# Reordering the start of a transformer-layer kernel: column groups, features and first products in the order in which their data lands

## The chip, the cores and the metric

The kernel runs on one core of one Trainium2 chip. The metric is the device time of one execution in microseconds; the time before is the median of three runs. The engines are TensorE (PE, with its weight loads listed as PEld), VectorE (DVE), ScalarE (ACT), GpSimd (POOL) and SyncE (SP), which issues the DMAs.

## The reference

One layer works on 512 latent tokens `x` and 256 context tokens `ctx`, both of width 1024, in f32. Only the new `x` is returned.

```python
mod   = silu(c)     @ w_ada + b_ada        # per channel shift, scale, gate for x
mod_c = silu(c_ctx) @ w_ada + b_ada        # the same for ctx
h  = rms_norm(x,   g_norm1) * (1 + sc1)  + sh1
hc = rms_norm(ctx, g_norm1) * (1 + csc1) + csh1
aq, ak, av, dq, dk, dv, dz, da, db, ga, gd = split_cols(h  @ w_in)
caq, cak, ...                              = split_cols(hc @ w_in)
...   # windowed attention and gated DeltaNet, merged, output projection, MLP
```

What matters here is the beginning: the modulation columns, the two norms, the modulated features `h` and `hc`, and the first column tiles of the product with `w_in`.

## The kernel before

Tokens lie along the free axis and channels along the partitions: the width of 1024 is eight channel tiles of 128 partitions, `kt` = 0 to 7. A product of one 128-column tile of `w_in` with all tokens is a sum over the eight channel tiles, over 512 columns of `x` and 256 of `ctx`. To keep f32 accuracy, weights and features are each split in a rounded upper part and a remainder, and `mm3` multiplies three pairs (L309 upper with upper, L310 upper with remainder, L311 remainder with upper). The split of a weight is `wload`: a DMA to a raw buffer (L251), the upper part on ScalarE (L256), the remainder on VectorE (L261). The raw buffers are two, so a third load waits until the first is split.

The start consists of these pieces:

- 36 warm-up matmuls of a tile of ones (L198), whose result nobody reads.
- For each channel tile the column group `ada(kt)`: two halves of 512 KB of `w_ada` are loaded (L215), and four small matmuls each (L217) form the rows of scale and shift. `columns(kt)` copies them (L231, ScalarE), turns them into columns (L236, TensorE) and adds the bias (L244, L245, VectorE) to get `modA` and `modS`. For tile 0 another 14 matmuls without a use stand behind it (L240).
- The norms: for `x` and then `ctx`, squares on ScalarE (L285), sums on VectorE (L289, L293), a sum over partitions as a matmul with ones (L296), and a logarithm and an exponent on ScalarE (both L156 through `act`). The program has all squares, then both exponents.
- The features of a channel tile, `modulate`: a product on VectorE (L314), the rounded upper part on ScalarE (L315), the remainder on VectorE (L316), for `x` and then for `ctx`.
- Three early weights (`load_early`: the gate tile and two key tiles), whose products are formed channel tile by channel tile as features come (`early`), into six of the eight banks of accumulation memory.

The instructions are not run in the order in which the program is written. A scheduler orders those of each engine by priority and readiness in its own estimate and sets the semaphores; the resulting order of every engine is fixed before the run, and each engine waits in it. An order can be forced by adding a dependency without a semaphore. SP issues DMAs in order too, and an issue also waits until the DMA eight places ahead of it has landed.

Behind the early products come the other tiles of `w_in` out of a queue of weights (`wnext`), with the gate steps, convolution, norms, attention and DeltaNet work in between, then merge, output projection and MLP.

## Time and profile before

| | |
|---|---|
| median of 3 runs | 920.05 us (916.64 to 921.29) |
| profiled execution | 919.03 us, span 917.3 us |
| mean granted TensorE clock | 0.996 |
| TensorE busy | 892.9 us, 97% of the span |
| VectorE, ScalarE, GpSimd busy | 648.8, 497.5, 26.0 us |

The span runs from the first to the last instruction; the execution's time holds 1.7 us more. In a timeline row stand the start, the duration, the engine, the line, the operation with output and inputs, and how many instructions the row merges; in brackets the idle time ahead of it and what ended it. Matmul durations overlap, since matmuls are pipelined; the distance of two starts is what one costs. A 128-column f32 matmul with an f32 operand counts as two rows. In the view of stretches stand the stretch, its length and for each engine its busy time with the number of instructions, then the granted TensorE clock (1.00 is full), the DMA engines' busy share and GB/s.

### The profile page before, as it was taken

Reading aid. Unit: us, or ns where it says so; the run is one execution under the profiler, and the core shown is the slowest. Engines: PE = TensorE matmul, PEld = TensorE weight load, DVE = VectorE, ACT = ScalarE, POOL = GpSimd, SP = SyncE. Lnnn points to the kernel's source line nnn. Section 1 sums busy time; section 2 is a strip of 40 time slices with the busy share of each in tenths; the row PEclk is TensorE's granted clock in tenths of the full one; section 3 lists DMA queues with packets and bytes.
Section 4 is the critical chain, followed back from the end, with each engine's and each line's share of the span. In section 5 each row is a group of like instructions: output and inputs, shape, how many; then the busy total and the mean of one; then the engine's idle time right before and its main releaser. Section 6 shows DMA issues by size and latency. Waiting matters only on the chain.

```text
span 917.3 us, 19321 instructions
## 1 busy us (share of the span) xinstructions
PE 892.9 (97%) x8228; PEld 748.7 (82%) x8228; DVE 648.8 (71%) x1100; ACT 497.5 (54%) x873; POOL 26.0 (3%) x42
## 2 busy tenths in 40 slices
PE   8999999999999999999999999999999999999998
PEld 6688677877777777878878889888899899889986
DVE  4665799966777998357787967997587477637731
ACT  5468755457768787485545425563265146414520
POOL 0000001010000001000000000000000000000000
PEclk9999999999999999999999999999999999999999
DMA  8914345442212133324455555453412340233031
GB/s 343 346 47 116 74 107 111 103 93 47 58 28 43 47 105 115 97 72 163 139 174 179 184 177 184 141 181 114 138 47 93 115 160 27 90 113 117 25 115 46
DMA packets 31910, 107.19 MB, mean 117 GB/s; under 512 B 3920, under 2 KB 4432, under 8 KB 31824
## 3 DMA queue, kind: packets, MB, share of 16 engines
q1 hardware_dynamic: 29520, 97.57, 31.4%
q0 software_dynamic: 2304, 8.39, 5.6%
q8 instruction: 64, 1.05, 0.5%
q14 instruction: 22, 0.18, 0.1%
HBM read 103.85 MB, written 2.10 MB: 116 GB/s over the span
## 4 chain that ended last, share of the span: by engine, by line
PE 81%; DVE 8%; ACT 7%; issue 2%; DMA 2%; SPq 0%; ACTq 0%; DVEq 0%
PE banks L309 14%; PE banks L310 14%; PE banks L311 14%; PE banks L988 11%; PE banks L1436 11%; PE banks L1034 2%; PE banks L1099 2%; ACT m L156 2%; PE banks L1111 1%; DMA m<-in_wm 1%; PE banks L1130 1%; PE banks L573 1%; DVE m L193 1%; PE banks L636 1%; PE banks L744 1%
## 5 line engine op out<-in xcount | busy, mean ns | idle before, releaser
L309 PE MATMUL banks<-m,wh 128*128 128x512 f32 (+1 forms) x568 | 212.8, 376 | 0.1
L310 PE MATMUL banks<-m,wh 128*128 128x512 f32 (+1 forms) x568 | 211.1, 372 | 0.0
L311 PE MATMUL banks<-m,wl 128*128 128x512 f32 (+1 forms) x568 | 210.8, 371 | 0.0
L256 ACT ACTIVATE wh<-wr 128x1024 fp32r<-128x1024 f32 (+1 forms) x92 | 90.5, 985 | 134.0 <-PE banks L310 113.1
L1436 PE MATMUL banks<-m,m 128*128 128x256 f32 x1008 | 123.6, 284 | 1.8 <-DVE m L193 1.0
L1436 PEld LDWEIGHTS banks<-m,m 128*128 128x128 f32 x1008 | 121.9, 192 | 3.6 <-DVE m L193 1.7
L311 PEld LDWEIGHTS banks<-m,wl 128*128 128x128 f32 x568 | 107.3, 189 | 18.8 <-issue 0.8
L309 PEld LDWEIGHTS banks<-m,wh 128*128 128x128 f32 x568 | 107.3, 189 | 18.5 <-ACT m L156 0.5
L192 ACT ACTIVATE m<-m 128x512 fp32r<-128x512 f32 (+2 forms) x118 | 82.5, 720 | 73.2 <-PE banks L1436 13.4
L310 PEld LDWEIGHTS banks<-m,wh 128*128 128x128 f32 x568 | 107.4, 189 | 17.5 <-DVE m L193 0.3
L193 DVE TENSOR_TENSOR m<-m,m 128x512 fp32r<-128x512 f32 (+2 forms) x118 | 92.3, 804 | 21.4 <-ACT m L192 16.8
L988 PE MATMUL banks<-m,wh 128*128 128x512 f32 x320 | 104.4, 400 | 0.6 <-ACT m L156 0.6
L261 DVE TENSOR_TENSOR wl<-wr,wh 128x1024 fp32r<-128x1024 f32 (+1 forms) x76 | 84.2, 1109 | 26.2 <-ACT wh L256 24.0
L1563 DVE SCALAR_TENSOR_TENSOR m<-banks,modT,m 128x512 f32<-128x512 f32 x32 | 24.0, 749 | 77.7 <-PE banks L311 77.7
L988 PEld LDWEIGHTS banks<-m,wh 128*128 128x128 f32 x320 | 59.3, 188 | 13.0 <-ACT m L156 0.8
L988 PE MATMUL banks<-m,wl 128*128 128x512 f32 x160 | 64.5, 403 | 0.0
L1053 DVE SCALAR_TENSOR_TENSOR m<-m,m 128x1024 f32<-128x1024 f32 x32 | 38.9, 1219 | 12.3 <-DMA m<-in_wada 12.2
L310 PE MATMUL banks<-m,m 128*128 128x256 f32 (+1 forms) x136 | 46.1, 346 | 0.1
L309 PE MATMUL banks<-m,m 128*128 128x256 f32 (+1 forms) x136 | 44.9, 344 | 1.2 <-ACT m L256 0.6
L311 PE MATMUL banks<-m,m 128*128 128x256 f32 (+1 forms) x136 | 44.8, 338 | 0.1
L988 PEld LDWEIGHTS banks<-m,wl 128*128 128x128 f32 x160 | 30.1, 188 | 6.2
L156 ACT ACTIVATE m<-banks,st 128x512 f32<-128x512 f32 (+1 forms) x32 | 23.5, 738 | 20.1 <-DVE st L530 19.8
(256 smaller groups left out, 1382.2 us busy)
## 6 DMA issues: line engine op xcount, KB each, us to landing
m<-in_wada SPq DMA_DIRECT2D x48, 512.0 KB, 5.0
wr<-in_wm SPq DMA_DIRECT2D x40, 512.0 KB, 3.4
wr<-in_win SPq DMA_DIRECT2D x39, 512.0 KB, 3.3
m<-in_wm SPq DMA_DIRECT2D x24, 512.0 KB, 3.4
wl<-in_win POOLq DMA_DIRECT2D x16, 512.0 KB, 5.5
m<-in_xT SPq DMA_DIRECT2D x8, 512.0 KB, 5.4
wr<-in_wbr SPq DMA_DIRECT2D x16, 256.0 KB, 2.7
wr<-in_wout SPq DMA_DIRECT2D x8, 512.0 KB, 3.3
```

Source lines behind the costliest of these rows:

```text
L156: r = A.activation(out_, in_, func, **kw)
L192: A.activation(r32(hi), src, AF.Copy)
L193: (eng or V).tensor_tensor(r32(lo), src, hi, op=ALU.subtract)
L256: A.activation(r32(hi), raw, AF.Copy)
L261: V.tensor_tensor(r32(lo), raw, hi, op=ALU.subtract)
L309: PE.matmul(acc, w[0][:, k, :], xhi, start=(start and i == 0), stop=False)
L310: PE.matmul(acc, w[0][:, k, :], xlo, start=False, stop=False)
L311: PE.matmul(acc, w[1][:, k, :], xhi, start=False, stop=(stop and i == n - 1))
L988: PE.matmul(acc.ap, w[x][:, k, :], hx[k][y], start=(k == p == 0), stop=(k == KT - 1 and p == 2))
L1053: V.scalar_tensor_tensor(wa.ap, wa.ap, 0.5, scr.ap, op0=ALU.mult, op1=ALU.mult, accum_out=modT[:, grp, j:j + 1])
L1436: PE.matmul(dst, r32(self.w[w][i][:, k * P:(k + 1) * P]), xs7[x][k][j], start=(n == 0), stop=(n == 11))
L1563: V.scalar_tensor_tensor(xn_[ct], accs[ct].ap, modT[:, 3, ct:ct + 1], xn_[ct], op0=ALU.mult, op1=ALU.add)
```

## The change

The same work is written in another order, with fewer warm-ups, and a few orders are forced.

- The warm-ups are 30 and 8 instead of 36 and 14.
- The DMA of the first early weight is issued ahead of those of `ctx`, and its upper part on ScalarE is forced behind the exponent of `x`.
- The norm of `x` is finished, exponent included, before the norm of `ctx`; the squares of `ctx` on ScalarE are forced behind the first rounded feature of `x`.
- Each partition sum of a norm is forced behind the column group's matmuls issued last.
- The feature of `x` of channel tile 0 is made ahead of column group 1, and the first early product of `x` (three matmuls) is placed behind it; the second partition sum is forced behind that product. Features of `ctx` are made once its norm is there.

```diff
-NONES, NWAIT = 36, 14
+NONES, NWAIT = 30, 8
...
+    def follow(later, earlier):
+
+        tc.add_manual_dep(later.ins, earlier.ins.name, nosync, reason="order")
...
-                PE.matmul(rp_[32 * g:32 * g + 32, :256], scond[:, half * 4 + g], wb[:, g * 256:(g + 1) * 256],
-                          start=(half == 0), stop=(half == 1))
+                last[0] = PE.matmul(rp_[32 * g:32 * g + 32, :256], scond[:, half * 4 + g], wb[:, g * 256:(g + 1) * 256],
+                                    start=(half == 0), stop=(half == 1))
...
-            PE.matmul(mp[:, half, :], rb_[:, half * P:(half + 1) * P], prm[:, 184:186], start=True, stop=True)
+            last[0] = PE.matmul(mp[:, half, :], rb_[:, half * P:(half + 1) * P], prm[:, 184:186], start=True, stop=True)
...
-        A.activation(r32(hi), raw, AF.Copy)
+        upper[0] = A.activation(r32(hi), raw, AF.Copy)
...
-    columns(0, ada(0))
+    rp0 = ada(0)
+    load_early()
+    w0 = upper[0]
     for k4 in range(KT // 4):
         nc.sync.dma_start(out=cs_[:, k4 * 1024:(k4 + 1) * 1024], in_=I["ctxT"][k4])
-    load_early()
...
-    for src, nt, n, r in ((xs_, 4, SEQ, rx), (cs_, 2, CTX, rc)):
+    def norm1(src, nt, n, r, sq_after=None):
         tot = None
         for i in range(nt):
             b = alloc(1024)
-            A.activation(b.ap, src[:, i * 1024:(i + 1) * 1024], AF.Square)
+            q = A.activation(b.ap, src[:, i * 1024:(i + 1) * 1024], AF.Square)
+            if sq_after:
+                follow(q, sq_after)
...
-        PE.matmul(ss[:, :n], ones, tot[:, :n], start=True, stop=True)
+        follow(PE.matmul(ss[:, :n], ones, tot[:, :n], start=True, stop=True), last[0])
         tot.free()
         act(r, ss[:, :n], AF.Ln, bias=epsc, scale=1.0 / D)
         ss.free()
-    for r in (rx, rc):
-        act(r, r, AF.Exp, scale=-0.5)
...
+        return act(r, r, AF.Exp, scale=-0.5)
...
-    for kt in range(1, AHEAD):
-        columns(kt, ada(kt))
-        load_early()
-    for kt in range(KT):
+
+    def features(kt):
+
         t = alloc(768)
         o, oc = kt * 1024, kt * 512
-        hx.append(modulate(t[:, :512], xt[kt], rx, modA[:, kt, 0:1], modS[:, kt, 0:1],
-                           H[:, o:o + 512], H[:, o + 512:o + 1024]))
-        hc.append(modulate(t[:, 512:768], ct_[kt], rc, modA[:, kt, 1:2], modS[:, kt, 1:2],
-                           HCb[:, oc:oc + 256], HCb[:, oc + 256:oc + 512]))
+        if len(hx) == kt:
+            hx.append(modulate(t[:, :512], xt[kt], rx, modA[:, kt, 0:1], modS[:, kt, 0:1],
+                               H[:, o:o + 512], H[:, o + 512:o + 1024]))
+        if len(normed) == 2:
+            hc.append(modulate(t[:, 512:768], ct_[kt], rc, modA[:, kt, 1:2], modS[:, kt, 1:2],
+                               HCb[:, oc:oc + 256], HCb[:, oc + 256:oc + 512]))
         t.free()
+
+    def early_x(w, acc, k):
+        return mm3(acc[:, :512], w, [hx[k]], start=(k == 0), stop=(k == KT - 1), ks=[k])
+
+
+    normed = [norm1(xs_, 4, SEQ, rx)]
+    follow(w0, normed[0])
+    columns(0, rp0)
+    features(0)
+    hi0 = upper[0]
+    columns(1, ada(1))
+    load_early()
+    low0 = early_x(*early[0], 0)
+    follow(low0, last[0])
+    last[0] = low0
+    normed.append(norm1(cs_, 2, CTX, rc, hi0))
+    for kt in range(KT):
+        features(kt)
         if kt + AHEAD < KT:
             columns(kt + AHEAD, ada(kt + AHEAD))
         if len(early) < len(EARLY):
             load_early()
         for (w, acc), k0 in zip(early, EARLY.values()):
             for k in range(kt + 1) if kt == k0 else (kt,):
-                mm3(acc[:, :512], w, [hx[k]], start=(k == 0), stop=(k == KT - 1), ks=[k])
+                if k or acc is not early[0][1]:
+                    early_x(w, acc, k)
                 mm3(acc[:, 512:768], w, [hc[k]], start=(k == 0), stop=(k == KT - 1), ks=[k])
```

`mm3` and `modulate` are moved up unchanged, except that `mm3` returns its last matmul and `modulate` remembers its ScalarE instruction in `upper`; `last` and `upper` hold the instruction issued last of their kind. The line numbers in the prediction are those of the kernel before.

More of the change, by code (lines that the diff above doesn't have):

```diff
@@ L216, in ada @@
             for g in range(4):
-                PE.matmul(rp_[32 * g:32 * g + 32, :256], scond[:, half * 4 + g], wb[:, g * 256:(g + 1) * 256],
-                          start=(half == 0), stop=(half == 1))
+                last[0] = PE.matmul(rp_[32 * g:32 * g + 32, :256], scond[:, half * 4 + g], wb[:, g * 256:(g + 1) * 256],
+                                    start=(half == 0), stop=(half == 1))
             wb.free()
         return rp_
+    last = [None]
     xs_, cs_ = alloc(8 * SEQ), alloc(8 * CTX)
@@ L246, in columns @@
         mp_.free()
+    upper = [None]
     def wload(src, n=KT, bufs=None, late=False):
@@ L270, in load_early, with mm3, modulate @@
         early.append((wload(I["win"][list(EARLY)[len(early)]], bufs=bb), bank(2)))
-    columns(0, ada(0))
+    def mm3(acc, w, xs, start=True, stop=True, ks=None):
+        ks = list(range(len(xs))) if ks is None else ks
+        n = len(ks)
+        for i, k in enumerate(ks):
+            xhi, xlo = xs[i]
+            PE.matmul(acc, w[0][:, k, :], xhi, start=(start and i == 0), stop=False)
+            PE.matmul(acc, w[0][:, k, :], xlo, start=False, stop=False)
+            r = PE.matmul(acc, w[1][:, k, :], xhi, start=False, stop=(stop and i == n - 1))
+        return r
+    def modulate(t, src, r, sc, sh, hi, lo, eng=V):
+        V.scalar_tensor_tensor(t, src, sc, r, op0=ALU.mult, op1=ALU.mult)
+        upper[0] = A.activation(r32(hi), t, AF.Identity, bias=sh)
+        eng.scalar_tensor_tensor(r32(lo), t, sh, hi, op0=ALU.add, op1=ALU.subtract)
+        return r32(hi), r32(lo)
+    rp0 = ada(0)
+    load_early()
+    w0 = upper[0]
     for k4 in range(KT // 4):
         nc.sync.dma_start(out=cs_[:, k4 * 1024:(k4 + 1) * 1024], in_=I["ctxT"][k4])
-    load_early()
     xt = [xs_[:, k * SEQ:(k + 1) * SEQ] for k in range(KT)]
@@ L299, in tile_layer @@
         ss.free()
-    for r in (rx, rc):
-        act(r, r, AF.Exp, scale=-0.5)
-    def mm3(acc, w, xs, start=True, stop=True, ks=None):
-        ks = list(range(len(xs))) if ks is None else ks
-        n = len(ks)
-        for i, k in enumerate(ks):
-            xhi, xlo = xs[i]
-            PE.matmul(acc, w[0][:, k, :], xhi, start=(start and i == 0), stop=False)
-            PE.matmul(acc, w[0][:, k, :], xlo, start=False, stop=False)
-            PE.matmul(acc, w[1][:, k, :], xhi, start=False, stop=(stop and i == n - 1))
@@ L313, in modulate @@
-    def modulate(t, src, r, sc, sh, hi, lo, eng=V):
-        V.scalar_tensor_tensor(t, src, sc, r, op0=ALU.mult, op1=ALU.mult)
-        A.activation(r32(hi), t, AF.Identity, bias=sh)
-        eng.scalar_tensor_tensor(r32(lo), t, sh, hi, op0=ALU.add, op1=ALU.subtract)
-        return r32(hi), r32(lo)
+        return act(r, r, AF.Exp, scale=-0.5)
     H, HCb = alloc(8 * 1024, True), alloc(8 * 512, True)
     hx, hc = [], []
-    for kt in range(1, AHEAD):
-        columns(kt, ada(kt))
-        load_early()
```

## The prediction

> **What bounds the kernel now.** I read the page first (the engines' shares, the chain that ended last), then the busy time by stretches of the first 60 us, then the timeline there; and beside them the order in which each engine holds its instructions in the two programs.

> ```profile
> span 917.3 us, 19321 instructions
> PE 892.9 (97%) x8228; PEld 748.7 (82%) x8228; DVE 648.8 (71%) x1100; ACT 497.5 (54%) x873; POOL 26.0 (3%) x42
> PE 81%; DVE 8%; ACT 7%; issue 2%; DMA 2%; SPq 0%; ACTq 0%; DVEq 0%
> ```

> TensorE is busy for 97% of the span and carries 81% of the chain. So a change off TensorE pays only where TensorE has nothing to do, and that is the start:

> ```profile
> 10.00:15.00 5.00, 3.75 (x32) 1.93 (x30) 2.59 (x3) 1.62 (x4) 0.00 (x0) 1.00 1.02 419
> 20.00:25.00 5.00, 3.79 (x24) 1.48 (x16) 2.44 (x7) 2.23 (x5) 0.00 (x0) 1.00 0.91 330
> 25.00:30.00 5.00, 5.00 (x31) 2.87 (x31) 3.10 (x5) 2.49 (x5) 0.00 (x0) 0.66 1.01 412
> 28.00:29.00 1.00, 1.00 (x10) 0.52 (x3) 0.10 (x1) 0.38 (x2) 0.00 (x0) 0.50 1.00 410
> ```

> The columns after the stretch are PE, PEld, DVE, ACT, POOL, then granted clock, DMA share, GB/s. Weight loads fill only 1.48 of the 5 us from 20 on: TensorE waits there. From about 26 to 29 us it ran at half clock. At 419 GB/s a transfer of 512 KB takes 1.25 us. Nothing later differs: behind the first features and their products all engines hold the same instructions in the same order in both programs. The whole effect is how much earlier TensorE becomes continuously busy with needed work.

> The timeline of before's start, engine by engine:

> ```profile
> 1.06 10.45 PE L198 MATMUL banks<-ones 128*128 128x128 f32 x72 [1.06 <-DVE ones L166]
> 9.57 1.06 ACT L285 ACTIVATE m<-m 128x1024 f32<-128x1024 f32 x1 [0.15 <-DMA m<-in_xT]
> 11.44 0.64 PE L217 MATMUL banks<-m,m 128*32 128x256 f32 x8
> 12.88 1.10 PE L296 MATMUL banks<-m,ones 128*128 128x512 f32 x2 [0.80 <-DVE m L293]
> 13.90 0.64 PE L217 MATMUL banks<-m,m 128*32 128x256 f32 x8
> 14.01 0.69 ACT L156 ACTIVATE m<-banks,epsc 128x512 f32<-128x512 f32 x1 [3.38 <-PE banks L296]
> 14.61 0.38 ACT L231 ACTIVATE m<-banks 128x256 f32<-128x256 f32 x1
> 14.89 1.05 ACT L285 ACTIVATE m<-m 128x1024 f32<-128x1024 f32 x1
> 15.05 0.61 PE L236 MATMUL banks<-c_prm,m 128*128 128x2 f32 x4 [0.50 <-ACT m L231]
> 15.51 3.37 PE L240 MATMUL banks<-m,ones 128*128 128x128 f32 x28
> 15.84 0.62 ACT L156 ACTIVATE m<-m 128x512 f32<-128x512 f32 x1
> 16.36 1.04 ACT L285 ACTIVATE m<-m 128x1024 f32<-128x1024 f32 x1
> 16.49 0.75 DVE L314 SCALAR_TENSOR_TENSOR m<-m,modA,m 128x512 f32<-128x512 f32 x1 [0.32 <-ACT m L156]
> 17.30 0.71 ACT L315 ACTIVATE m<-m,modS 128x512 fp32r<-128x512 f32 x1
> 17.43 1.23 DVE L289 TENSOR_TENSOR m<-m,m 128x1024 f32<-128x1024 f32 x1 [0.19 <-ACT m L285]
> 17.91 1.04 ACT L256 ACTIVATE m<-wr 128x1024 fp32r<-128x1024 f32 x1
> 18.58 0.75 DVE L316 SCALAR_TENSOR_TENSOR m<-m,modS,m 128x512 fp32r<-128x512 f32 x1
> 19.01 0.51 PE L309 MATMUL banks<-m,m 128*128 128x512 f32 x1
> 19.24 1.22 DVE L261 TENSOR_TENSOR m<-wr,m 128x1024 fp32r<-128x1024 f32 x1
> 19.38 0.50 PE L310 MATMUL banks<-m,m 128*128 128x512 f32 x1
> 20.38 1.14 DVE L293 TENSOR_TENSOR m<-m 128x512 f32<-128x512 f32 x2
> ```

> The reader sees a hand-off chain. The last quarter of x lands at 9.57. The column group of tile 0 runs in halves around the sum of squares (L296), its second half only at 13.90. ScalarE squares ctx at 14.89 and 16.36, in front of the exponent, the feature and the first weight split that TensorE awaits. Consecutive ScalarE rows overlap by about 0.1 us.

> **Warm-ups.** L198 falls from 36 matmuls to 30, L240 from 14 to 8 (two rows each). The 28 rows of L240 take 3.37 us, 0.12 each; 12 fewer save 1.44 us in either place. The first saving is worth nothing by itself: column group 0 lands at 9.57 + 1.25 = 10.8 and, one transfer on, 12.1, later than the warm-ups then end (11.44 - 1.44 = 10.0). It does let both halves run as they land, in front of L296, which stays at 12.88 because VectorE's sum holds it. The second matters in the next step.

> **First product of x.** L231 moves ahead of the logarithm, about 12.7 to 13.1. L236 follows L296 at 13.9 instead of 15.05; eight warm-ups end near 16.3. The logarithm stays at 14.01; with no squares of ctx behind it the exponent runs 14.7 to 15.4. The weights, queued in front of ctx, land at 12.1 + 1.25 = 13.3. ScalarE splits them 15.3 to 16.35. VectorE's product (0.75) ends at 16.15, the rounded feature runs 16.3 to 17.0, and the first L309 starts at 17.0 instead of 19.01. VectorE's weight remainder (1.22) runs 16.4 to 17.6, the feature's remainder (0.75) to 18.35; L310 at 18.4 instead of 19.38.

> **What the move costs.** The squares of ctx now come after: 16.9 to 18.9. VectorE adds (1.23) to 20.15 and folds (1.14) to 21.2; the second L296 comes at 21.25. Before:

> ```profile
> 20.49 0.33 SPq L251 DMA_DIRECT2D wr<-in_win  x1
> 21.57 0.70 PE L296 MATMUL banks<-m,ones 128*128 128x256 f32 x2
> 22.31 0.47 ACT L156 ACTIVATE m<-banks,epsc 128x256 f32<-128x256 f32 x1 [3.35 <-PE banks L296]
> 23.33 0.61 PE L236 MATMUL banks<-c_prm,m 128*128 128x2 f32 x4 [0.49 <-ACT m L231]
> 24.88 0.51 ACT L315 ACTIVATE m<-m,modS 128x256 fp32r<-128x256 f32 x1 [0.35 <-DVE m L314]
> 27.47 1.08 PE L217 MATMUL banks<-m,m 128*32 128x256 f32 x8
> 29.50 0.50 PE L236 MATMUL banks<-c_prm,m 128*128 128x2 f32 x4
> 30.40 0.40 PE L309 MATMUL banks<-m,m 128*128 128x512 f32 x1
> 30.64 0.40 PE L310 MATMUL banks<-m,m 128*128 128x512 f32 x1
> 46.19 1.07 PE L217 MATMUL banks<-m,m 128*32 128x256 f32 x16
> 61.98 0.40 PE L309 MATMUL banks<-m,wh 128*128 128x512 f32 x1
> 62.71 0.50 PE L309 MATMUL banks<-m,wh 128*128 128x512 f32 x1
> ```

> So ctx's norm is 0.3 us early at worst, not late. What is queued behind it: its logarithm (22.0 to 22.5) stands on ScalarE in front of the feature of tile 1, which then runs 22.4 to 23.1; VectorE's remainders of weight 1 and feature 1 end at 23.5 and 24.2; the two ctx features of 0.5 us each pass VectorE, ScalarE, VectorE until 26.1.

> **Where TensorE is then.** Column group 1 lands at 17.1 and 18.3 and runs after L310 in one piece, 18.75 to 19.8 (16 rows take 1.07, row at 46.19); L231 is done at 20.2 and L236 comes at 20.3 instead of 23.33. L296 ends at 21.95, then products interleave with group 2; the last holds are feature 1 (23.1), weight remainder 1 (23.5) and feature remainder 1 (24.2). Group 2's second half ends at 25.4, and the L236 of tile 2 comes at 26.25 instead of 29.50: 3.25 us earlier. By the two orders TensorE has by then also done four more 512-column products (0.24 us from 30.40 to 30.64; I take 0.23) and two fewer of 256 columns (half of that): 4 x 0.23 - 2 x 0.115 = 0.69. Together 3.9 us ahead. From here on TensorE has work queued in both programs: before runs without a hole worth naming to 61.98, where the next stage's first product starts. So the lead stays.

> **The other queues.** On SP the weights pass two transfers of ctx, which land 1.25 us later, at 14.6 and 15.8, and are wanted at 16.9: free. If ScalarE came to them a full 1.25 us sooner, that is what it would cost. The third early weight's DMA waits for a raw buffer, 20.49 before; now for the remainder at 17.6: this ends the dip to 330 GB/s, worth nothing while column groups land ahead of use. At the other end SP now issues the triangle masks behind two weight loads, waiting for VectorE's last feature remainder; ScalarE's two roundings of them then stand behind the gate's first step. Their cover: the next weight's products, 8 x 3 x (0.23 + 0.115) = 8.3 us, read no mask. Between 61.98 and 62.71 TensorE waited for ScalarE's L156 to empty banks; that L156 now stands one eviction earlier, so 0.25 us of idle goes as well. Bounds of this stretch: -0.3 (gap gone) to +0.7 (the roundings hold the banks); I take -0.2, as the order shows L156 in front of the roundings.

> **Sum.** 3.9 + 0.2 = 4.1 us if the clock holds, less if it does not.

> **The clock.** Before drops to half at about 26 and recovers before 30, though TensorE's rows stood for 3.79 of the 5 us ahead of it. The same can fall on the sparse stretch of the new order, 16.3 to 19: two single products and the start of group 1 in it. Price: rows of L217 at half clock (27.47) took 1.08 for 8 rows where 16 take 1.07 warm, so group 1 would end near 20.5, its L236 come at 21.0, and L296 near 21.9 instead of 21.25: 0.7 us, the rest being covered by VectorE's folds until 21.2. If it never drops, nothing is lost; the bounds are 0 and 0.7, I take the middle, 0.3: gain 3.8 us. [...]

> The profiled execution took 919.03 us (span 917.3 and 1.7 around it); 919.03 - 3.8 = 915.2. The median shown is 920.05, 1.0 above it, so **916.2** on that footing.

> **Rivals.** About 0.5% (4.6 us) is what a measurement of this kernel can tell from no change.
> (1) *The lead as worked out*, 2 to 4.6 us: 915.5 to 918. Chance 0.58.
> (2) *A larger lead.* Before's half clock around 28 was paid in needed work; if the new order keeps full clock and the three last holds (23.1, 23.5, 24.2) come a few tenths earlier, TensorE saturates by 24 instead of 26 and the lead is 5 to 6 us: 914 to 915. For it: every hand-off was taken at its before length. Against: the holds stand in series on ScalarE and VectorE. Chance 0.28.
> (3) *The lead arrives and is given back*: masks and gate steps on ScalarE, or the weight load behind the masks on SP, are late for the stage behind 61.98. For it: ScalarE's order there does change, one eviction of 256 columns moves behind four gate steps. Against: the projection that needs those banks starts only behind the 8.3 us above. 919 to 920. Chance 0.09.
> (4) *Slower*: the thinner warm-ups leave the clock at half from 19 on for three stretches like that of 26 to 29.4 instead of one. My order holds about 5 us of TensorE work between 19 and 25.9: doubled, less 1.5 of waiting that it covers, 3.5 us, which eats the lead; a third stretch of 3.4 us costs 1.7 to 3 more: 922 to 923. It decides from the second stretch on. Against: from 22 on products are denser than before's. Chance 0.05.
> That the edits do nothing is excluded by the two orders.

> The range for 8 in 10 takes in (1), most of (2) and the near end of (3): 912.9 to 920.0. Faster by over 0.5% (under 915.4) 0.28, same 0.67, slower 0.05.

> **What would show it.** In the changed profile: first L309 of a feature near 17.0; the second tile's L236 near 20.3 and the third's near 26.2; the next stage's first product on a pool weight near 58, not 61.98; no SP stall to 20.5; the granted clock in 19 to 23. The prediction fails if that product comes near 58 and the span does not follow (3), or if the granted clock is half for more than 4 us (4).

## The result and the profile after

The changed kernel takes 924.64 us (median of 10 runs, 920.67 to 927.16) against 919.0 us of before beside it: ratio 1.0052, 95% interval 1.0028 to 1.0077. It is slower, by about 0.5%; 916.2 had been forecast. Its profiled execution took 923.57 us, with a mean granted clock of 0.992 (before 0.996).

Line numbers move with each edit: L309, L310 and L311 of before are L286, L287 and L288 after, L236 is L242, L296 is L325, L744 is L776 and L1099 is L1131; kernels with a further loop in front have these two lines more, or four.

The page of the changed kernel, with the lines that answer to those shown of before:

```profile
span 921.8 us, 19277 instructions
PE 892.6 (97%) x8204; PEld 749.1 (81%) x8204; DVE 649.2 (70%) x1100; ACT 497.9 (54%) x873; POOL 26.1 (3%) x42
PE 79%; DVE 8%; ACT 6%; DMA 3%; issue 3%; SPq 0%; DVEq 0%; ACTq 0%
```

TensorE holds 24 rows and 24 weight loads fewer, the twelve warm-ups. In the chain, "issue" (waiting for nothing that the profile shows) rises from 2% to 3% of a span that is longer.

The start, from the timelines of TensorE and SP of the changed kernel:

```profile
16.97 0.50 PE L286 MATMUL banks<-m,m 128*128 128x512 f32 x1 [0.77 <-ACT m L293]
17.60 0.33 SPq L259 DMA_DIRECT2D wr<-in_win  x1
18.29 0.51 PE L287 MATMUL banks<-m,m 128*128 128x512 f32 x1 [0.81 <-DVE m L294]
20.38 0.61 PE L242 MATMUL banks<-c_prm,m 128*128 128x2 f32 x4 [0.50 <-ACT m L237]
21.32 0.70 PE L325 MATMUL banks<-m,ones 128*128 128x256 f32 x2
26.13 0.51 PE L242 MATMUL banks<-c_prm,m 128*128 128x2 f32 x4
57.97 0.40 PE L286 MATMUL banks<-m,wh 128*128 128x512 f32 x1
```

Every row lies within about 0.1 us of the prediction: the next stage starts at 57.97 instead of 61.98. So the lead of 4.0 us arrived. What became of it is seen at the same VectorE instructions in the two timelines, first of before, then of the changed kernel:

```profile
81.83 0.32 DVE L700 COPY gtok<-banks 128x96 f32<-128x96 f32 x1
118.96 0.69 DVE L774 TENSOR_TENSOR m<-m,m 128x512 f32<-128x512 f32 x1
133.10 0.69 DVE L774 TENSOR_TENSOR m<-m,m 128x512 f32<-128x512 f32 x1
191.08 0.75 DVE L619 SCALAR_TENSOR_TENSOR m<-banks,c_prm,m 128x511 f32<-128x511 f32 x1 [4.02 <-ACT m L618]
408.44 0.42 DVE L1141 TENSOR_TENSOR m<-m,banks 128x256 f32<-128x256 f32 x1 [1.34 <-ACT m L1121]
913.41 0.75 DVE L1563 SCALAR_TENSOR_TENSOR m<-banks,modT,m 128x512 f32<-128x512 f32 x1 [4.69 <-PE banks L311]
```

```profile
77.68 0.32 DVE L732 COPY gtok<-banks 128x96 f32<-128x96 f32 x1
117.25 0.69 DVE L806 TENSOR_TENSOR m<-m,m 128x512 f32<-128x512 f32 x1 [2.47 <-ACT m L156]
134.13 0.69 DVE L806 TENSOR_TENSOR m<-m,m 128x512 f32<-128x512 f32 x1 [1.39 <-ACT m L156]
190.57 1.14 DVE L651 SCALAR_TENSOR_TENSOR m<-banks,c_prm,m 128x511 f32<-128x511 f32 x2 [2.94 <-ACT m L650]
412.23 0.42 DVE L1173 TENSOR_TENSOR m<-m,banks 128x256 f32<-128x256 f32 x1 [2.00 <-PE banks L1162]
917.96 0.75 DVE L1595 SCALAR_TENSOR_TENSOR m<-banks,modT,m 128x512 f32<-128x512 f32 x1 [4.69 <-PE banks L288]
```

The changed kernel is 4.15 us ahead at 78, 1.71 ahead at 117, 1.03 behind at 134, again 0.51 ahead at 191, 3.79 behind at 412 and 4.55 behind at the end. The engines' orders are the same there; the time goes in two stretches, 108 to 134 and about 400 to 409. TensorE's timeline shows what stands in them. First before, its only such row, then the changed kernel:

```profile
116.03 0.83 PE L744 MATMUL banks<-m 64*32 64x32 f32 x73 [2.09 <-issue]
```

```profile
113.25 0.90 PE L776 MATMUL banks<-m 64*32 64x32 f32 x49 [3.26 <-issue]
129.51 1.29 PE L776 MATMUL banks<-m 64*32 64x32 f32 x85 [1.74 <-issue]
403.33 3.23 PE L1131 MATMUL banks<-m,m 64*64 64x64 f32 x60 [2.76 <-issue]
```

In the middle of a long burst of tiny matmuls (64x32 and 64x64 products of the DeltaNet's chunks) TensorE stops, and the profile shows nothing that holds it. In the changed kernel it stops three times, for 7.76 us together, in the kernel before once for 2.09. In the first burst 73 rows remain behind the hole before and 49 after: a difference of 24, the number of warm-up rows removed. Counted from the start, the first hole stands at the same place in both, behind 1114 rows and 1114 weight loads (the stretch from 0 to 116 us of before, then from 0 to 113 us of the changed kernel):

```profile
0.00:116.00 116.00, 108.90 (x1114) 83.88 (x1114) 72.32 (x139) 74.40 (x116) 5.28 (x10) 0.99 0.56 185
0.00:113.00 113.00, 104.59 (x1114) 81.02 (x1114) 73.97 (x141) 75.45 (x118) 5.29 (x10) 1.00 0.58 192
```

And behind the holes the clock drops (stretches of the changed kernel; the column behind POOL is the granted clock):

```profile
114.00:116.00 2.00, 2.00 (x15) 1.55 (x7) 0.75 (x2) 0.00 (x0) 0.00 (x0) 0.50 0.04 10
130.00:132.00 2.00, 2.00 (x61) 1.74 (x53) 1.97 (x2) 0.71 (x2) 0.00 (x0) 0.50 0.28 57
404.00:406.00 2.00, 2.00 (x44) 2.00 (x42) 0.42 (x1) 1.94 (x4) 0.00 (x0) 0.50 0.04 8
```

Before has 1.00 in each of these. It has a half clock of its own elsewhere, behind a wait of TensorE for ScalarE of 1.95 us that ends at 145.40; that is where the changed kernel gets ahead again:

```profile
146.00:148.00 2.00, 2.00 (x5) 1.07 (x4) 1.93 (x7) 1.59 (x3) 0.71 (x1) 0.50 0.00 0
```

The page's table of DMA queues, which the prediction did not use, names a suspect (packets, MB, share of 16 engines); the second row is the same queue between 109 and 113 us of the changed kernel:

```profile
q8 instruction: 64, 1.05, 0.5%
q8 instruction: 1, 0.02, 3.9%
```

```profile
108.81 1.18 PE L776 MATMUL banks<-m 64*32 64x32 f32 x117
```

At that pace a piece of them, 128 rows, is used up in an estimated 1.3 us, sooner than the next one comes when that takes 2.5 us.

### The profile page after: what moved, and what is told of

It reads as the page before. It is cut to its first block, busy times and chain, and to the rows that moved or that the text cites. A ratio compares the mean times of both kernels' runs of the same rounds, so it can differ in the third digit from the quotient of the medians.

```text
span 921.8 us, 19277 instructions
## 1 busy us (share of the span) xinstructions
PE 892.6 (97%) x8204; PEld 749.1 (81%) x8204; DVE 649.2 (70%) x1100; ACT 497.9 (54%) x873; POOL 26.1 (3%) x42
## 3 DMA queue, kind: packets, MB, share of 16 engines
q8 instruction: 64, 1.05, 0.5%
## 4 chain that ended last, share of the span: by engine, by line
PE 79%; DVE 8%; ACT 6%; DMA 3%; issue 3%; SPq 0%; DVEq 0%; ACTq 0%
PE banks L286 14%; PE banks L287 14%; PE banks L288 14%; PE banks L1468 10%; PE banks L1020 9%; PE banks L1066 2%; PE banks L1131 2%; DMA m<-in_wm 2%; ACT m L156 2%; PE banks L776 1%; PE banks L605 1%; PE banks L1143 1%; PE banks L1162 1%; PE banks L668 1%; DMA m<-in_wada 1%
## 5 line engine op out<-in xcount | busy, mean ns | idle before, releaser
L286 PE MATMUL banks<-m,wh 128*128 128x512 f32 (+1 forms) x568 | 213.0, 376 | 0.0
L287 PE MATMUL banks<-m,wh 128*128 128x512 f32 (+1 forms) x568 | 211.5, 372 | 0.0
L288 PE MATMUL banks<-m,wl 128*128 128x512 f32 (+1 forms) x568 | 210.8, 371 | 0.0
L288 PEld LDWEIGHTS banks<-m,wl 128*128 128x128 f32 x568 | 107.4, 189 | 18.6 <-issue 0.5
L286 PEld LDWEIGHTS banks<-m,wh 128*128 128x128 f32 x568 | 107.4, 189 | 18.3 <-ACT m L156 0.4
L287 PEld LDWEIGHTS banks<-m,wh 128*128 128x128 f32 x568 | 107.6, 189 | 17.7 <-DVE m L197 0.3
L196 ACT ACTIVATE m<-m 128x512 fp32r<-128x512 f32 (+2 forms) x118 | 82.6, 720 | 72.3 <-PE banks L1468 16.3
L1020 PEld LDWEIGHTS banks<-m,wh 128*128 128x128 f32 x320 | 59.3, 188 | 13.1 <-ACT m L156 0.8
L286 PE MATMUL banks<-m,m 128*128 128x256 f32 (+1 forms) x136 | 44.9, 344 | 1.3 <-ACT m L293 1.2
L287 PE MATMUL banks<-m,m 128*128 128x256 f32 (+1 forms) x136 | 45.2, 341 | 0.9 <-DVE m L294 0.8
L288 PE MATMUL banks<-m,m 128*128 128x256 f32 (+1 forms) x136 | 44.5, 336 | 0.0
L156 ACT ACTIVATE m<-banks,st 128x512 f32<-128x512 f32 (+1 forms) x32 | 23.5, 739 | 22.3 <-DVE st L562 22.1
```

The costliest lines, as they stand in the source:

```text
L156: r = A.activation(out_, in_, func, **kw)
L196: A.activation(r32(hi), src, AF.Copy)
L286: PE.matmul(acc, w[0][:, k, :], xhi, start=(start and i == 0), stop=False)
L287: PE.matmul(acc, w[0][:, k, :], xlo, start=False, stop=False)
L288: r = PE.matmul(acc, w[1][:, k, :], xhi, start=False, stop=(stop and i == n - 1))
L1020: PE.matmul(acc.ap, w[x][:, k, :], hx[k][y], start=(k == p == 0), stop=(k == KT - 1 and p == 2))
```

## The experiments

**Theory A, the pieces.** Twelve warm-ups less are 48 instructions less (24 rows and 24 loads by the two pages), so every later piece ends 24 rows further on in the work. A burst that starved little starves more, and the clock drops behind it. By this theory only the count modulo 256 matters. **Rival B, the phase.** The lead itself brings bursts, transfers and clock into another phase. A third reading came up later: more instructions ahead help by themselves.

### Two parts of the change taken apart

The new order with the old warm-ups, and the old order with the new ones:

```diff
-NONES, NWAIT = 30, 8     # the changed kernel
+NONES, NWAIT = 36, 14
```

> The new order with the old 36 and 14 warm-ups, all else in the order of the changed kernel. Theory A (instruction supply: TensorE's instructions come in pieces of 16 KB, 256 of them, and where a piece ends inside a dense burst decides the stall; 12 warm-ups fewer are 48 instructions fewer ahead of every burst): the burst of small products near 110 us stalls 2.1 us as before, not 3.3, the second burst and the one near 400 us do not stall, the lead of about 4 us stays, 914.5 to 916.5. Theory B (the 4 us lead itself puts the bursts onto other transfers or another phase of the clock): the stalls and half clock stay as in the changed kernel, 923 to 925.

```diff
-NONES, NWAIT = 36, 14    # the kernel before
+NONES, NWAIT = 30, 8
```

> The kernel before with 30 and 8 warm-ups alone. Theory A: no lead, but the stalls of the changed kernel (3.3, 1.7 and 2.8 us in place of 2.1, 0 and 0, with half clock behind them): 924 to 929, slower than the changed kernel. Theory B: no lead, so the stalls of before, 918 to 920.

The new order with 36 and 14 took 916.26 us (ratio 0.9956, 0.9939 to 0.9973), the old order with 30 and 8 took 925.91 us (1.0075, 1.005 to 1.0099). TensorE's holes, first of the former, then of the latter:

```profile
111.58 0.83 PE L776 MATMUL banks<-m 64*32 64x32 f32 x73 [1.39 <-issue]
130.51 0.50 PE L288 MATMUL banks<-m,wl 128*128 128x512 f32 x1 [1.59 <-issue]
```

```profile
116.06 0.90 PE L744 MATMUL banks<-m 64*32 64x32 f32 x49 [3.15 <-issue]
131.30 0.93 PE L744 MATMUL banks<-m 64*32 64x32 f32 x85 [2.17 <-issue]
```

The number of rows left, 73 or 49, goes with the warm-ups, not with the order, and so do the long holes. The latter kernel also has the third hole, 1.60 us before the same 60 rows at 404.08; the former has a second one of 1.59 us, at another row, which theory A had not expected. The loss is in the warm-up counts. B falls: with the same lead and the old counts 3.3 us of it are left at the end (919.53 beside it).

### Instructions without work

Twelve, then 32 matmuls of 32 columns (four instructions each) put behind the first warm-ups of the changed kernel:

```diff
     for _ in range(NONES):
         PE.matmul(wb_[:, :P], ones, ones, start=True, stop=True)
+    for _ in range(12):      # 32 in the second run
+        PE.matmul(wb_[:32, :32], ones[:64, :32], ones[:64, :32], start=True, stop=True)
```

> The changed kernel with 12 tiny matmuls (32 columns, half the rows) behind the first warm-ups, 48 instructions, some 0.3 us in a place where TensorE waits for a transfer. Theory A: as with the old warm-ups, 914.5 to 916.5, and the pieces end at the same instructions as in the kernel before. Theory B, or that the wide warm-ups mattered for the clock: 923 to 925.

> The changed kernel with 32 tiny matmuls, 128 instructions, half a piece. Theory A: the pieces end half a piece away from those of the changed kernel, the stalls move to other bursts or change length; the time is another than 924.6 by more than 2 us, in a direction that I cannot work out. Theory B: 923 to 925.

Twelve took 918.39 us (0.9983, 0.9966 to 1.0), 32 took 919.31 us (0.9996, 0.9979 to 1.0012); both are faster than the changed kernel, to which they only add work. With 12 the time is above the 914.5 to 916.5 expected by theory A; what is missing is sought below. The first burst's hole with 12, and with 32:

```profile
113.69 0.83 PE L778 MATMUL banks<-m 64*32 64x32 f32 x73 [1.65 <-issue]
```

```profile
112.04 1.16 PE L778 MATMUL banks<-m 64*32 64x32 f32 x113 [1.29 <-issue]
```

73 rows again, and 49 + 64 = 113: the 24 and 64 added rows, with their loads, pulled the end of the piece forward by exactly 24 and 64 rows.

### One whole piece

26 and 4 warm-ups with 40 and 32 tiny matmuls behind them: 256 instructions more than the changed kernel.

```diff
-NONES, NWAIT = 30, 8
+NONES, NWAIT = 26, 4
...
+    for _ in range(40):      # behind the first; 32 behind the second
+        PE.matmul(wb_[:32, :32], ones[:64, :32], ones[:64, :32], start=True, stop=True)
```

> The changed kernel with 26 and 4 warm-ups and, without a use, 40 and 32 tiny matmuls (32 columns) behind the first and the second of them: 256 TensorE instructions more than the changed kernel, one whole piece, and the same work behind. Instruction pieces (A): the ends of the pieces lie on the same rows as in the changed kernel, so the first burst stands before its last 49 rows for about 3 us, the second before its last 85 for about 2 us, the third before its last 60 for about 2.8 us, the granted clock drops behind them, and the time is 922 to 926 us, although there are more warm-ups than ever. More instructions ahead help by themselves (B): 12 and 32 tiny matmuls took 5 to 6 us off, so 72 give 916 to 920 us. The piece ends follow from the count alone by A; how long each hole lasts may shift by some tenths with the time of the fetch.

922.25 us (1.0034, 1.0015 to 1.0053): slower than before again.

```profile
114.09 0.90 PE L780 MATMUL banks<-m 64*32 64x32 f32 x49 [3.70 <-issue]
130.11 0.93 PE L780 MATMUL banks<-m 64*32 64x32 f32 x85 [2.09 <-issue]
402.69 3.32 PE L1135 MATMUL banks<-m,m 64*64 64x64 f32 x60 [3.10 <-issue]
```

49, 85 and 60 rows, as in the changed kernel. Ahead of the first hole stand 1242 rows and as many loads, 128 of each more than the 1114; in the twelve other profiles of this text it is 1114 each time. The period that this run shows is 256 instructions; that more instructions help by themselves is excluded. The pages agree that the queue counts instructions: it has 65 packets in the three kernels with 80 or 208 more than before, 64 in all others.

### Which warm-ups keep the clock at the start

The 12 tiny matmuls have the piece ends of 36 and 14, and yet took 2.1 us more. The two kernels between 20 and 24 us, first 36 and 14, then 30 and 8 with the 12 tiny ones:

```profile
20.00:24.00 4.00, 3.26 (x23) 1.83 (x20) 3.93 (x8) 2.72 (x5) 0.00 (x0) 1.00 1.03 418
```

```profile
20.00:24.00 4.00, 3.52 (x17) 2.53 (x17) 3.15 (x6) 2.35 (x4) 0.00 (x0) 0.50 1.02 418
```

So six of the twelve were made wide again, late or early, and six left tiny:

```diff
-NONES, NWAIT = 30, 8
+NONES, NWAIT = 30, 14    # or 36, 8
...
+    for _ in range(6):
+        PE.matmul(wb_[:32, :32], ones[:64, :32], ones[:64, :32], start=True, stop=True)
```

> 30 and 14 warm-ups and 6 tiny matmuls behind the first 30: the instruction count of the old counts, so the same piece ends as with 36 and 14 (918.4 with 30, 8 and 12 tiny ones; 916.3 with 36 and 14). If the second, later warm-ups are what keeps the clock full from 16 to 26 us, the granted clock there is 1.00 and the time about 916.3 us; if the first 30 or 36 matter, half clock from 20 to 26 us as with the 12 tiny ones and about 918.4 us.

> 36 and 8 warm-ups and 6 tiny matmuls behind the first 36: again the piece ends of the old counts. If the later warm-ups keep the clock, there are too few of them here: half clock at 20 to 26 us and about 918.4 us. If the first ones matter: full clock there and about 916.3 us. The piece ends (last 73 rows of the first burst) are the same in both cases.

916.08 us (0.9961, 0.9945 to 0.9977) and 916.56 us (0.9961, 0.9942 to 0.998). Both keep 1.00 from 20 to 26 us, which neither alternative foresaw: six more in either place do. Both are, like the one with 36 and 14, faster than either kernel.

### One transfer less

GpSimd sums some weight remainders by transfer; one of them, issued at 108 us, runs while the first burst's piece is fetched. Here that weight is split on VectorE.

```diff
-    wq = [lambda a=a, i=i: wload(*a, late=LODMA[0] <= i < LODMA[1]) for i, a in enumerate(wq)]
+    wq = [lambda a=a, i=i: wload(*a, late=LODMA[0] <= i < LODMA[1] and i != 6) for i, a in enumerate(wq)]
```

> The changed kernel with one weight (the seventh of the queue) not summed by a transfer that GpSimd issues at 108 us, but split on VectorE as the first weights are: the instruction count stays. If the hole of the first burst was long because its instruction piece (109.5 us, about 2.5 us long) shared the DMA engines with that transfer, the packet takes about 1 us, the hole is 1.3 to 1.8 us instead of 3.3, the clock behind it stays full or drops less, and the run is 1.5 to 4 us faster than the changed kernel: 920 to 923 us. If the length of the hole does not depend on the transfer, it stays near 3.3 us and the time near 924.6, or above by the 1.2 us more on VectorE. The second and third hole are as in the changed kernel in both cases.

922.83 us (1.0037, 1.0015 to 1.006); the interval overlaps that of the changed kernel, so a gain is not shown. The queue between 112 and 116 us, and the hole:

```profile
q8 instruction: 1, 0.02, 1.4%
114.85 0.63 PE L776 MATMUL banks<-m 64*32 64x32 f32 x49 [2.11 <-issue]
```

The piece now takes 1.4% x 16 x 4 = 0.9 us instead of 2.5, with no other packet beside it, and the hole is 2.11 us instead of 3.26 before the same 49 rows. It is shorter as expected, but not the 1.3 to 1.8 us, and the clock dropped behind it all the same (0.91 from 100 to 120). The second and third holes were 1.42 and 2.46 us. The edit also moved a few matmuls and VectorE instructions nearby.

With 36 and 14 the same transfer was there, and the piece took only 1.0 us. The two met differently. There GpSimd issued the transfer at 108.52 and the fetch began at 109.28, 0.8 us later, when hardly any of its packets had started; in the changed kernel the issue was at 108.11 and the fetch began at 109.51, 1.4 us later, among them. The transfer's queue while the piece was fetched, first in the changed kernel (109.5 to 112 us), then with 36 and 14 (109.25 to 110.25):

```profile
q0 software_dynamic: 88, 0.36, 89.5%
q0 software_dynamic: 8, 0.03, 29.4%
```

So it is in all twelve profiles with this transfer: in the five with the changed kernel's count modulo 256 the fetch began 1.4 to 1.6 us behind the issue and took 2.2 to 2.65 us, in the seven others 0.4 to 1.0 us behind it and took 0.9 to 1.4. That a transfer under way lengthens this fetch is thus well supported; the one run that removes it moved other work too.

### The two causes combined, and the changed kernel again

30 and 14 with 26 tiny matmuls (the count of the run with 32 tiny ones, the warm start), 24 and 14 (the count of the changed kernel, six of the warm-ups later), and the changed kernel once more:

```diff
-NONES, NWAIT = 30, 8
+NONES, NWAIT = 30, 14    # and range(26) tiny ones behind the first
```

```diff
-NONES, NWAIT = 30, 8
+NONES, NWAIT = 24, 14
```

> 30 and 14 warm-ups and 26 tiny matmuls behind the first 30: the instruction count of the run with 32 tiny ones (919.3 us), but the warm start of the run with 30 and 14 (916.1 us). If the piece ends and the clock at the start together set the time, the piece ends are those of the former (the first burst stands before its last 113 rows, for about 1.3 us), the start is that of the latter (full clock from 20 to 26 us, the copy of the gates' projection on VectorE at 77.4 to 78.1 us), and the time is 915 to 917 us. If the tiny matmuls as such cost the time there, it is 918.5 to 920 us.

> 24 and 14 warm-ups: as many as in the changed kernel (38), and so its piece ends, but six of them later. If the holes behind the piece ends are the loss, they stand before the same 49, 85 and 60 rows, for 3, 2 and 2.8 us, and the run is slower than before: 921 to 924 us, a bit under the changed kernel where the later ones keep the clock full at 20 to 26 us. If the first stretch's clock were the main loss of the changed kernel, the run would be faster than before: 916 to 918 us.

> The changed kernel once more, beside the two others on the same chip: by the pieces 922 to 926 us with holes before 49, 85 and 60 rows of the three bursts. The clock from 20 to 26 us may be full (as in its first profile) or half (as in the profile of the variant without one transfer), worth 2 to 2.7 us at the copy of the gates' projection (77.7 against 79.9 to 80.4 us).

918.0 us (0.9979, 0.9957 to 1.0001), 923.67 us (1.0055, 1.0034 to 1.0075) and 925.61 us (1.0066, 1.0038 to 1.0093). The holes of 24 and 14, then of the changed kernel:

```profile
115.26 0.90 PE L776 MATMUL banks<-m 64*32 64x32 f32 x49 [3.23 <-issue]
129.43 0.93 PE L776 MATMUL banks<-m 64*32 64x32 f32 x85 [1.13 <-issue]
401.60 3.47 PE L1131 MATMUL banks<-m,m 64*64 64x64 f32 x60 [1.65 <-issue]
```

```profile
114.88 0.90 PE L776 MATMUL banks<-m 64*32 64x32 f32 x49 [2.95 <-issue]
131.41 1.39 PE L776 MATMUL banks<-m 64*32 64x32 f32 x85 [2.05 <-issue]
405.12 3.47 PE L1131 MATMUL banks<-m,m 64*64 64x64 f32 x60 [2.79 <-issue]
```

The rows left are the same in every profile of this count; the lengths differ by up to 1.1 us between these two. Two expectations missed here. The first kernel was 1 us over its range. Its profile had full clock from 20 to 26 and holes of 1.55, 1.81 and 0.60 us, but it is of the fastest of twelve executions (914.91 us, granted clock 1.0); ten of the others had 0.995 to 0.998, and where they lost it no profile shows. And 24 and 14 did not keep the clock: it had 0.59 from 16 to 20. Its first warm-ups end at 8.85 us, 1.8 us ahead of the next matmul; that this is why is likely, not shown. Of the changed kernel this second profile had half clock at the start, where the first had none:

```profile
20.00:24.00 4.00, 3.50 (x17) 2.36 (x9) 2.94 (x6) 1.81 (x4) 0.00 (x0) 0.50 1.02 419
79.62 0.32 DVE L732 COPY gtok<-banks 128x96 f32<-128x96 f32 x1
```

The copy that came at 77.68 then comes at 79.62: 1.9 us.

By instruction count all kernels stand so (difference to before, modulo 256; a number behind a plus is of tiny matmuls):

| count | kernels | us | rows left, first burst |
|---|---|---|---|
| 0 | old order | 919.0 to 919.5 | 73 |
| 0 | new order, 36/14; 30/14 + 6; 36/8 + 6; 30/8 + 12 | 916.3; 916.1; 916.6; 918.4 | 73 |
| +80 | new order, 30/8 + 32; 30/14 + 26 | 919.3; 918.0 | 113 |
| -48 | new order, 30/8 (twice); 24/14; 26/4 + 72; 30/8 with one transfer less | 924.6, 925.6; 923.7; 922.3; 922.8 | 49 |
| -48 | old order, 30/8 | 925.9 | 49 |

## Why the prediction was wrong, point by point

**The start: right.** Forecast and measured: L309 17.0 and 16.97, L310 18.4 and 18.29, L296 21.25 and 21.32, the L236 of tiles 1 and 2 20.3 and 20.38, 26.25 and 26.13, the next stage 58 and 57.97. SP's third early load came at 17.60, as said. The masks of rival (3) cost nothing: the lead is 4.01 us at 58 and 4.15 at 78. With the old counts the new order gives 916.26, the forecast 916.2, but that is chance: this is the order alone, the forecast was for both changes, and the gain over the 919.53 beside it is 3.3 us, not 3.8.

**"Nothing later differs. [...] So the lead stays": this step failed.** The engines' orders are the same, but TensorE's instructions came in pieces (64 packets of 16.4 KB on q8), and where the first burst's piece ended had moved by 24 rows, from 73 to 49 rows ahead of the burst's end. The lead of 4.15 us at 78 us became 4.55 us of delay: 8.70 us lost. In the first two bursts it is 5.18 us, of which the holes account for 3.26 + 1.74 - 2.09 = 2.91; in the third it is 4.30, the hole 2.76. The rest there, 2.27 and 1.54 us, goes with the clock (stretches of the changed kernel; before has 1.00 in both):

```profile
108.00:134.00 26.00, 20.57 (x511) 15.96 (x498) 19.88 (x31) 10.01 (x16) 1.73 (x2) 0.80 0.41 91
400.00:409.00 9.00, 6.24 (x124) 5.42 (x112) 3.40 (x8) 5.53 (x10) 1.04 (x2) 0.81 0.21 62
```

Taken as a mix of 1.00 and 0.50, 0.80 over 26 us and 0.81 over 9 are 10.4 and 3.4 us at half clock, worth up to 5.2 and 1.7 us if TensorE was busy in all of it: enough for the rest. Between the second and the third burst the changed kernel gained 1.54 us, where before waits and runs at half clock around 145 us; 0.76 us more went behind the third.

**"12 fewer save 1.44 us in either place": priced as time alone.** A warm-up was also four instructions (twelve fewer are 24 rows and 24 loads fewer), and more of them went with a full clock: with six of the twelve back in either place it was 1.00 from 20 to 24 us, with twelve tiny ones in their stead 0.50, with none of the twelve 1.00 in one profile and 0.50 in another. With 36 and 14 the copy at 78 comes at 78.08 instead of 77.68: where the clock held, the fewer warm-ups bought 0.4 us. The instructions were not in the sum at all; the chain of waits showed "issue 2%" and the queue table 64 packets of instructions, and the prediction used neither.

**The clock term: too small.** I bounded it by 0 and 0.7 us and took 0.3. The first profile had no drop there (0 us), the second had one from about 19 to 25 us, worth 1.9 us at the copy at 78; with one transfer less the same copy came at 80.42, 2.7 us late. In the new order with 30 and 8, with or without tiny matmuls or the transfer, four of five profiles show it (all but the first of the changed kernel). TensorE's longest hole ahead of it in the second profile was 0.98 us, at 10.8. So a drop came here behind no hole longer than that; what sets it off is not shown. The two profiles are of the same kernel: 1.00 from 20 to 24 us in the first, 0.50 in the second.

**The rivals.** (4) had the right sign, 922 to 923 us, and half clock in it, but its place was the start and its cause the thinner warm-ups' activity; the measured loss stands behind 100 us and comes from the instruction pieces. In the second profile its sign, half clock for more than 4 us at the start, did come, and it cost 1.9 us, not the lead. (3), the lead given back, is what happened in outline, with another mechanism, and more than the lead was lost. "That the edits do nothing is excluded by the two orders" holds; that the orders tell everything does not.

## What to carry to other kernels

An order that is the same on every engine is not the same program in time: TensorE's instructions came in pieces of 256 here, and a piece that ended inside a dense burst of tiny matmuls cost up to 3.7 us (3.70 with one whole piece more), with a half clock behind 15 of the 20 holes longer than 1.60 us. When an edit adds or removes instructions ahead of such bursts, count them modulo the piece seen in the trace, 256 here, and look at the rows released by "issue" in both timelines and at the transfers beside the fetch; judge the edit with the count held fixed. A few matmuls without a use moved the ends here at little cost (twelve tiny ones are 24 rows, at 0.01 us each an estimated 0.24 us, and the changed kernel went from 924.64 to 918.39 us with them); whether they help has to be measured.

## What the runs showed of the hardware

**The length of a hole.** At the first burst a piece took from 0.9 us (the changed kernel with 32 tiny matmuls) to 2.65 us (one whole piece more). In the changed kernel it began at 109.5 and ended at 112.0, and the hole lasted from 109.99 to 113.25: TensorE ran dry 0.5 us after the fetch began and went on 1.25 us after it ended. With 36 and 14 the fetch began at 109.28 and took 1.0 us, and the hole lasted from 110.19 to 111.58: dry 0.9 us after the beginning, on 1.3 us after the end. At this burst TensorE went on 1.0 to 1.5 us after the end in all thirteen profiles; it ran dry 0.25 to 0.5 us after the beginning with the changed kernel's count, 0.65 to 0.95 with the others. So at this burst where a piece ended went with how much work was left when the next was fetched, 0.25 to 0.5 us or 0.65 to 0.95, and with whether the fetch fell among a transfer's packets; the fetch's own length, 0.9 to 2.65 us, did the rest.

**Half clock behind holes.** The nine "issue" holes of 2.46 us or more in these profiles were all followed by half clock; none of 1.60 us or less was; between them it went both ways (two of 1.65, 1.74, 2.05, 2.11 and 2.17 dropped; 1.67, 1.81, 2.00 and two of 2.09 did not). No threshold follows from that.

**Warm-ups.** In the new order 30 and 14 or 36 and 8 (with tiny ones) kept the clock full from 20 to 26 us in each of three profiles, 30 and 8 in one of five. That more of them, which nobody waits for, are worth 2 us was not expected.
